# A two-layer decoder trunk on one core: the norms before the query projections rearranged, and two parts of x loaded through the chunk buffers

## The chip, the core and the metric

The kernel runs on one core of a Trainium2 chip. Its time is the device time of one execution in microseconds (us); for a program on one core that is the core's own. Lower is better.

The engines are named as in the profile: PE is TensorE (matrix products; PEld is its loading of weights), DVE is VectorE, ACT is ScalarE, POOL is GpSimd, SP is SyncE, which here only issues transfers. A line such as L293 is line 293 of the kernel before. The changed kernel's lines lie 2 to 25 further down.

## The reference

The input is 256 tokens of width 1024, in float32. Two layers follow each other. Each layer has a token mixer (layer 0 an mLSTM, layer 1 an RG-LRU) beside cross-attention to 256 memory tokens, an output projection, a layer norm, a PEER mixer (a choice among 16384 experts, by query projections and sub-keys), and a second layer norm:

```
for i in range(DEPTH):
    z = x @ w_in[i]
    ...
    mix = concat([mixer(z), cross_attention(z, mem)]) @ w_out[i]
    x = layer_norm(alpha * x + mix, ln1_g[i], ln1_b[i])
    y = peer_ffn(x, peer_w_q[i], peer_subkeys[i], peer_u[i], peer_v[i])
    x = layer_norm(alpha * x + y, ln2_g[i], ln2_b[i])
```

`peer_ffn` begins with `x @ w_q` (1024 to 2048 columns). The norm of concern is the first one of each layer: it stands between the output projection `w_out` and the query projection `w_q`.

## The kernel before

**Precision by splitting.** Every float32 matrix product is made of three products of a rounded type (`mm3`, L166 to L169): each operand is split into a high part H (a cast, ScalarE) and a low part L = value - H (a subtraction, VectorE or GpSimd), and H*H, H*L and L*H are summed in a PSUM bank. One weight chunk (128 rows of a weight, up to 1024 columns) thus gives 24 products of 256 columns in a query projection: eight tiles of 128 columns, three products each.

**The chunk stream.** `plan` lists all weights as chunks in the order of their use. `load` issues their transfers on SyncE's queue into five chunk buffers (`raw`), and `pump` splits the next chunks into three pairs `wH`, `wL`: the cast on ScalarE (L97), and the subtraction either on GpSimd alone (L110), or for the first `pool_cols` columns on GpSimd and for the rest on VectorE (L112). `next()` hands out the split of a chunk and pumps those ahead of it. The gains and biases of a norm (g and b) are chunks too and occupy two of the five buffers until the norm releases them.

**The start.** The first eight chunks of the list are the parts of the transposed x, in turn with the first weight's chunks. A part of x isn't loaded into a chunk buffer but into a piece of `qT` (`to.stage`), a tile that is used for something else later and lies in the memory that two tiles of the setup have used before. The first weight chunks come in two pieces each.

**The norm before the query projection.** `proj_n` runs the last output-projection products in an order written out by hand: those of the first 128 tokens (tt = 0), then those of the second (tt = 1), in three column pieces. Between them the generator `norm` is stepped; it is called with `early` here. For tt = 0 it adds and normalises while the products of tt = 1 run, on VectorE, ScalarE and GpSimd (`scale_beside`, L305 to L309), splits two chunks of the query projection ahead with GpSimd alone doing the low parts (`pool_cols = D`), and turns the first four blocks of 128 columns into the transposed layout (`turn`: transposes on TensorE at L319, high part at L222, low part at L223). For tt = 1 the end of the statistics comes after the last product; then on VectorE: `center` (L293) and `spread` (L298) of the first 256 columns, `turn(1, 0, 1)` for two blocks, and only then the query projection's first product can start. Behind that VectorE does the remaining columns (L293 and L298, 256 and then 512 wide). Their turns follow as side work (`rest`), one step at each later chunk. The norm at the end of layer 0 takes the path `fill`, that at the end of layer 1 the path `last`; neither goes through the lines changed below `if fill`.

**Engines' queues.** Each engine runs its own instructions in the order in which the program issues them (TensorE's weight loads may run ahead of its products), and waits where one depends on another engine.

Of the kernel before, what the change touches and what calls it, by code (L numbers as in the profile page):

```python
# [7 lines left out]
F32 = mybir.dt.float32  # L8
# [5 lines left out]
ALU = mybir.AluOpType  # L14
# [19 lines left out]
EXTRA = 3  # L34
MIX_COLS = 0
GAP = 56
CAND = [(0, 1, 16, 0), (1, 1, 8, 16), (2, 1, 5, 24), (3, 1, 4, 29), (4, 1, 3, 33), (5, 3, 2, 36), (8, 8, 1, 42)]
NCAND = 50
ROWS = [(16, 16), (24, 8), (29, 5), (33, 4), (36, 3), (38, 2), (40, 2), (42, 2)]
# [5 lines left out]
class Trunk:  # L45
# [31 lines left out]
    def pump(self, upto):  # L77
        nc = self.nc
        upto = min(upto, len(self.items))
        while self.n_split < upto:  # L80
            i = self.n_split
            self.load(i + 1)
            ap, n, dest, keep, cuts = self.items[i]
            r = self.loaded.pop(i)
            self.n_split += 1
            if keep is not None:
                self.kept[keep] = r
                continue
            if type(dest) is int:
                h, l = self.extra[dest]  # L90
            elif dest is None:
                h = self.hl.tile([P, D], F32R, name="wH")[:, :n]
                l = self.hl.tile([P, D], F32R, name="wL")[:, :n]
            else:
                h, l = dest()
            for c in cuts:
                (nc.vector.tensor_copy if self.cast_dve else nc.scalar.copy)(h[:, c], r[:, c])  # L97
            k = n if getattr(dest, "pool", False) else min(n, self.pool_cols)
            if len(cuts) > 1:
                for c in cuts:  # L100
                    e = (nc.vector, nc.gpsimd)[c.start > 0]
                    e.tensor_sub(l[:, c], r[:, c], h[:, c].bitcast(F32))
                k = n
            elif k and self.chained:
                nc.vector.tensor_sub(l[:, k:], r[:, k:], h[:, k:].bitcast(F32))  # L105
                k += 2
                nc.gpsimd.tensor_sub(l[:, :k], r[:, :k], h[:, :k].bitcast(F32))  # L107
                k = n
            elif k:
                nc.gpsimd.tensor_sub(l[:, :k], r[:, :k], h[:, :k].bitcast(F32))  # L110
            if k < n:
                nc.vector.tensor_sub(l[:, k:], r[:, k:], h[:, k:].bitcast(F32))  # L112
            self.split[i] = (h, l)
            self.n_flight -= getattr(dest, "stage", None) is None
            self.load(len(self.items))
# [42 lines left out]
            self.tick()  # L158

    pool_cols = MIX_COLS  # L160
    chained = False
    cast_dve = False

# [18 lines left out]
    def proj_n(self, splits, stat, order=range(DT), tail=0, hook=(-1, None)):  # L182
        sH, sL = stat
        parts = [splits, (512, 256, 256) if tail else splits]
        banks = [[self.bank() for _ in p] for p in parts]
        late = []

        def products(tt, k, late):
            t = slice(tt * P, (tt + 1) * P)
            w = parts[tt][k]  # L190
            c0 = sum(parts[tt][:k])
            for n_, dt_, (h, l) in late:
                self.mm3(banks[tt][k][:, :w], sH[:, dt_, t], sL[:, dt_, t], h[:, c0:c0 + w], l[:, c0:c0 + w],
                         n_ == 0, n_ == last[tt])
        last = (DT - 1, DT - 1 - HL_BUFS if tail else DT - 1)
        for n, dt in enumerate(order):
            if n == hook[0]:
                hook[1]()
            late.append((n, dt, self.next(min(HL_BUFS + min(n, EXTRA), DT - n) if tail else HL_BUFS)))
            if n + 1 > DT - tail and n + 1 < DT:  # L200
                continue
            if tail and n + 1 == DT:
                break
            for tt in range(2):
                for k in range(len(parts[tt])):
                    products(tt, k, late)
            late = []
        if not tail:
            return banks
        ln = self.norm(banks, False, True)  # L210
        own, ring = late[:tail - HL_BUFS], late[tail - HL_BUFS:]
        for part in (own, ring):
            for k in range(2):
                products(0, k, part)
        next(ln)
        for k in range(3):
            products(1, k, ring)
        for k in range(3):
            products(1, k, own), next(ln, None)

    def split_to(self, dH, dL, src, cast=None):
        (cast or self.nc.scalar.copy)(dH, src)  # L222
# [31 lines left out]
    def norm(self, y, last, early, fill=False):  # L254
# [40 lines left out]
        def spread(tt, q, n):  # L295
            qs = slice(q * Q, (q + n) * Q)
            xs = x[:, tt, qs]
            nc.vector.scalar_tensor_tensor(xs, xs, rs[:, tt:tt + 1], b[:, qs], op0=ALU.mult, op1=ALU.add)  # L298
# [12 lines left out]
        def store(eng, tt, q, n):  # L311
            qs = slice(q * Q, (q + n) * Q)
            eng.dma_start(self.out[tt * P:(tt + 1) * P, qs], x[:, tt, qs])

        def turn(tt, q, n):
            p = self.bank()
            for j in range(2 * n):
                dt = 2 * q + j
                nc.tensor.transpose(p[:, j * P:(j + 1) * P], x[:, tt, dt * P:(dt + 1) * P], self.ident)  # L319
            t = slice(tt * P, (tt + 1) * P)  # L320
            ds = slice(2 * q, 2 * q + 2 * n)
            self.split_to(self.xH[:, ds, t], self.xL[:, ds, t],
                          p[:, :2 * n * P].rearrange("p (a t) -> p a t", a=2 * n))
# [29 lines left out]
        if early:  # L353
            yield
            part = add(1, 0)
        half(*part)
        self.pool_cols = D
        self.pump(self.n_got + 2 + (2 if early else 1))
        self.pool_cols = MIX_COLS
        if early:  # L360
            turn(0, 0, 2)
# [15 lines left out]
            return  # L377
        center(1, 0, 1)
        root(1)
        spread(1, 0, 1)  # L380
        if not early:
            turn(0, 0, 1)
        turn(1, 0, 1)
        scale(1, 1, 1)
        scale(0, 2, 2), scale(1, 2, 2)
        self.release("g", "b")

        def rest():
            yield
            if not early:  # L390
                turn(0, 1, 1)
            turn(1, 1, 1)
            yield
            turn(0, 2, 2)
            yield
            turn(1, 2, 2)
# [751 lines left out]
    def plan(self):  # L1148
        A = self.A

        def w(name, n, dts=range(DT)):
            for dt in dts:
                self.add(A[name][dt], n)

        def part(name, dst, k):
            fl = lambda t: t[:, 2 * k:2 * k + 2, :].rearrange("p a b -> p (a b)")
            to = lambda: (fl(dst()[0]), fl(dst()[1]))
            to.pool = True
            self.add(A[name][k], 512, to)

        def first(name):
            w(name, 1024, range(3))
            for k in range(4):
                part("memT", lambda: self.mem, k)
                w(name, 1024, (3 + k,))
            w(name, 1024, (7,))

        def norm(n, layer):
            for k in "gb":
                ap = A[f"{n}_{k}"][layer]  # L1170
                self.add(bass.AP(tensor=ap.tensor, offset=ap.offset, ap=[[0, P], [1, D]]), D, None, k)

        def tail(layer):
            for i, dt in enumerate((6, 7, 0, 1, 2, 3, 4, 5)):
                self.add(A["w_out"][layer, dt], D, i - 2 if 0 <= i - 2 < EXTRA else None)
            norm("ln1", layer)
            for g in range(2):
                for dt in range(DT):
                    self.add(A["w_q"][layer, g, dt], D)
            for i in range(P):  # L1180
                self.add(A["u"][layer, i], D)
            for i in range(P):
                e = i - P + HL_BUFS + EXTRA
                self.add(A["v"][layer, i], D, e if layer and 0 <= e < EXTRA else None)
                k = (i - N0 - 4) // 6
                if layer == 0 and i > N0 and (i - N0 - 4) % 6 == 0 and 0 <= k < 8:
                    if k < 4:
                        part("memT", lambda: self.mem, k)
                    else:
                        self.add(A["wkv"][1, k - 4], D, lambda c=k - 4: self.kvw[c])  # L1190
            norm("ln2", layer)
        for dt in range(DT):
            to = lambda dt=dt: (self.xH[:, dt, :], self.xL[:, dt, :])
            to.stage = lambda dt=dt: self.qT[:, dt, :]
            self.add(A["xT"][dt // 2][:, dt % 2 * T:(dt % 2 + 1) * T], T, to)
            self.add(A["w0kg"][dt], 896, cuts=2 if dt < 2 else 1)
        first("w0qx")
        for c in range(4):
            self.add(A["wkv"][0, c], D)
        w("w0v", 768)  # L1200
        w("w0o", 768)
        tail(0)
        w("w1x", 1024)
        w("w1g", 768)
        tail(1)
# [87 lines left out]
```

## Time and profile before

| | us |
|---|---|
| median of 3 runs | 1838.18 |
| lowest and highest | 1837.2 and 1838.45 |
| the profiled execution | 1838.14 |
| its span, first to last instruction | 1836.4 |

| engine | busy us | share of the span |
|---|---|---|
| TensorE, products | 1806.4 | 98% |
| TensorE, weight loads | 1665.8 | 91% |
| VectorE | 1297.5 | 71% |
| ScalarE | 941.4 | 51% |
| GpSimd | 433.1 | 24% |

The trace numbers are start times from the span's beginning and durations, both in us; a line of the timeline reads: start, duration, engine, line of the kernel, operation, output and inputs, shapes, count, and in brackets the idle time before it with what ended it. A granted clock of 1.00 is TensorE's full clock. The norm before the query projection is at 127 to 148 us in layer 0 and at 1025 to 1046 us in layer 1.

### The profile page before, as it was taken

To read this page: it belongs to the slowest core of one execution; us is meant where nothing else is said; L and a number is where in the kernel's file an instruction comes from. 1 tells how busy PE (TensorE), PEld (TensorE's weight loads), DVE (VectorE), ACT (ScalarE), POOL (GpSimd) and SP (SyncE) were. 2 spreads that over 40 slices of the span, in tenths; PEclk is the share of its full clock that TensorE was granted. 3 is DMA by queue.
4 is the path that set the end of the run, shared out by engine and by line. 5 is a ranking of instruction groups with operands and counts; after the bars stand their busy time and mean duration, and the time that the engine had idled before them with its cause. 6 is when DMAs were issued, how large, how long until landed. Compare 5 with 4: busy or idle time off the path is not lost.

```text
span 1836.4 us, 33231 instructions
## 1 busy us (share of the span) xinstructions
PE 1806.4 (98%) x12756; PEld 1665.8 (91%) x12756; DVE 1297.5 (71%) x2652; ACT 941.4 (51%) x1608; POOL 433.1 (24%) x324
## 2 busy tenths in 40 slices
PE   8999999999999999999999899999999999999998
PEld 8999999999999888888898699999999988888886
DVE  5674669599998555666568648795999965555556
ACT  6554555455545444555547355554555455555443
POOL 2005772333331000000011368335333300000000
PEclk9999999999999999999999899999999999999999
DMA  6656566655555666667654355666555566666664
GB/s 235 208 158 187 173 186 194 195 172 162 161 161 164 192 196 193 195 217 226 209 186 133 118 174 183 192 196 187 161 162 161 162 182 194 193 192 193 194 194 137
DMA packets 95265, 334.21 MB, mean 182 GB/s; under 512 B 10621, under 2 KB 13697, under 8 KB 94849
## 3 DMA queue, kind: packets, MB, share of 16 engines
q1 hardware_dynamic: 93464, 328.93, 58.6%
q10 hardware_dynamic: 1640, 3.15, 0.5%
q8 instruction: 100, 1.64, 0.4%
q14 instruction: 61, 0.49, 0.1%
HBM read 330.98 MB, written 1.05 MB: 181 GB/s over the span
## 4 chain that ended last, share of the span: by engine, by line
PE 73%; issue 15%; POOL 7%; DVE 3%; ACT 2%; DMA 0%; POOLq 0%; DVEq 0%; SPq 0%; ACTq 0%
PE bank L167 23%; PE bank L169 23%; PE bank L168 23%; POOL wL L107 7%; PE bank L226 2%; ACT wH L97 1%; DVE wL L112 0%; PE bank L319 0%; DVE aa L765 0%; DVE xc L731 0%; POOL wL L110 0%; DVE st L278 0%; DVE x L272 0%; ACT pr L451 0%; DMA cp<-in_rg_par_dram 0%
## 5 line engine op out<-in xcount | busy, mean ns | idle before, releaser
L97 ACT CAST wH<-raw 128x1024 fp32r<-128x1024 f32 (+2 forms) x605 | 628.6, 1040 | 772.5 <-PE bank L169 323.3
L112 DVE TENSOR_TENSOR wL<-raw,wH 128x1024 fp32r<-128x1024 f32 (+3 forms) x410 | 464.1, 1134 | 452.1 <-ACT wH L97 451.4
L167 PE MATMUL bank<-xHL,wH 128*128 128x256 f32 x2536 | 717.5, 283 | 7.1 <-ACT wH L97 6.2
L169 PE MATMUL bank<-xHL,wL 128*128 128x256 f32 x2536 | 704.5, 278 | 2.2 <-DVE wL L112 2.2
L168 PE MATMUL bank<-xHL,wH 128*128 128x256 f32 x2536 | 704.6, 278 | 0.0
L167 PEld LDWEIGHTS bank<-xHL,wH 128*128 128x128 f32 x2536 | 479.5, 189 | 7.9 <-ACT wH L97 6.2
L169 PEld LDWEIGHTS bank<-xHL,wL 128*128 128x128 f32 x2536 | 479.3, 189 | 3.1 <-DVE wL L112 2.8
L168 PEld LDWEIGHTS bank<-xHL,wH 128*128 128x128 f32 x2536 | 479.9, 189 | 0.3 <-DVE xHL L223 0.3
L168 PE MATMUL bank<-wL,cH 128*128 128x512 f32 x1015 | 394.3, 388 | 0.0
L169 PE MATMUL bank<-wH,cL 128*128 128x512 f32 x1015 | 394.3, 388 | 0.0
L167 PE MATMUL bank<-wH,cH 128*128 128x512 f32 x1015 | 394.3, 388 | 0.0
L110 POOL TENSOR_TENSOR wL<-raw,wH 128x1024 fp32r<-128x1024 f32 (+1 forms) x121 | 259.1, 2145 | 212.8 <-ACT wH L97 212.2
L169 PEld LDWEIGHTS bank<-wH,cL 128*128 128x128 f32 x1015 | 190.5, 188 | 39.7
L167 PEld LDWEIGHTS bank<-wH,cH 128*128 128x128 f32 x1015 | 190.5, 188 | 39.4
L168 PEld LDWEIGHTS bank<-wL,cH 128*128 128x128 f32 x1015 | 190.5, 188 | 39.0
L107 POOL TENSOR_TENSOR wL<-raw,wH 128x386 fp32r<-128x386 f32 x126 | 129.6, 1029 | 280.0 <-DVE wL L105 280.0
L308 POOL TENSOR_TENSOR x<-x,raw 128x256 f32<-128x256 f32 x6 | 4.8, 805 | 556.7 <-ACT x L305 556.7
L929 DVE TENSOR_TENSOR oh<-iota,i12T 128x1024 f16<-128x1024 f16 x128 | 130.2, 1017 | 0.0
L105 DVE TENSOR_TENSOR wL<-raw,wH 128x640 fp32r<-128x640 f32 x126 | 103.9, 825 | 7.7
L932 DVE TENSOR_TENSOR oh<-oh,gT 128x1024 f16<-128x1024 f16 x128 | 90.0, 703 | 4.4
L1062 PE MATMUL bank<-oh 128*128 128x128 f16 x1024 | 80.9, 220 | 1.1 <-DVE oh L932 1.1
L1062 PEld LDWEIGHTS <-oh 128*128 128x128 f16 x1024 | 58.8, 97 | 6.0 <-DVE oh L932 1.5
(273 smaller groups left out, 1527.7 us busy)
## 6 DMA issues: line engine op xcount, KB each, us to landing
raw<-in_u_dram SPq DMA_DIRECT2D x256, 512.0 KB, 3.7
raw<-in_v_dram SPq DMA_DIRECT2D x256, 512.0 KB, 4.3
raw<-in_w_q_dram SPq DMA_DIRECT2D x32, 512.0 KB, 3.8
raw<-in_w_out_dram SPq DMA_DIRECT2D x16, 512.0 KB, 4.5
raw<-in_w0qx_dram SPq DMA_DIRECT2D x8, 512.0 KB, 4.8
raw<-in_wkv_dram SPq DMA_DIRECT2D x8, 512.0 KB, 4.7
raw<-in_w1x_dram SPq DMA_DIRECT2D x8, 512.0 KB, 4.5
raw<-in_w0v_dram SPq DMA_DIRECT2D x8, 384.0 KB, 6.1
```

Source lines behind the costliest of these rows:

```text
L97: (nc.vector.tensor_copy if self.cast_dve else nc.scalar.copy)(h[:, c], r[:, c])
L105: nc.vector.tensor_sub(l[:, k:], r[:, k:], h[:, k:].bitcast(F32))
L107: nc.gpsimd.tensor_sub(l[:, :k], r[:, :k], h[:, :k].bitcast(F32))
L110: nc.gpsimd.tensor_sub(l[:, :k], r[:, :k], h[:, :k].bitcast(F32))
L112: nc.vector.tensor_sub(l[:, k:], r[:, k:], h[:, k:].bitcast(F32))
L167: mm(out, sH, mH, start=start, stop=False, skip_group_check=True)
L168: mm(out, sH, mL, start=False, stop=False, skip_group_check=True)
L169: mm(out, sL, mH, start=False, stop=stop, skip_group_check=True)
L226: self.nc.tensor.matmul(out, lhsT, rhs, start=start, stop=stop, skip_group_check=True)
L929: nc.vector.tensor_tensor(flat(oh[:, 1:3]), self.iota2.unsqueeze(1).to_broadcast([P, 4, P, 2]), pairs(self.i12T[:, j]), op=ALU.is_equal)
L932: nc.vector.tensor_tensor(flat(oh[:, 0:2]), two.rearrange("p z (q e t) -> p z q e t", q=2, t=2), pairs(self.gT[:, j]), op=ALU.mult)
L1062: nc.tensor.matmul(wp[:, qs], oh[:, 2, q // 2, :, q % 2], oh[:, z, q // 2, :, q % 2], start=z == 0, stop=z == 1, skip_group_check=True)
```

## The change

1. In the norm, the second chunk that is split ahead has its low part halved: GpSimd does 512 columns, VectorE the other 512. VectorE's half is put off: it is recorded in a list (`owed`) and issued later, behind the first turn of tt = 1.
2. `spread` of the first 256 columns of tt = 1 is issued as two passes of 128 columns, and `turn1` turns the two blocks one by one: transpose, cast, transpose, cast into one PSUM bank, then the two low parts.
3. `idle` issues transposes of the identity into a bank that nobody reads: 20 ahead of `turn1`, five behind it.
4. The first two parts of x are loaded into chunk buffers and no longer into `qT`.
5. Branches for a norm that is neither `early`, `last` nor `fill` go; no norm of this kernel took them.

```
+FILL = (20, 5)
...
             if k < n:
-                nc.vector.tensor_sub(l[:, k:], r[:, k:], h[:, k:].bitcast(F32))
+                rest = lambda l=l, r=r, h=h, k=k: nc.vector.tensor_sub(l[:, k:], r[:, k:], h[:, k:].bitcast(F32))
+                self.put_off(rest) if self.put_off else rest()
...
+    put_off = None
...
+    def idle(self, n):
+        b = self.bank()
+        for _ in range(n):
+            self.nc.tensor.transpose(b[:, :P], self.ident, self.ident)
...
+        def turn1(tt, *dts):
+            p = self.bank()
+            t = slice(tt * P, (tt + 1) * P)
+            for j, dt in enumerate(dts):
+                nc.tensor.transpose(p[:, j * P:(j + 1) * P], x[:, tt, dt * P:(dt + 1) * P], self.ident)
+                nc.scalar.copy(self.xH[:, dt, t], p[:, j * P:(j + 1) * P])
+            for j, dt in enumerate(dts):
+                nc.vector.tensor_sub(self.xL[:, dt, t], p[:, j * P:(j + 1) * P], self.xH[:, dt, t].bitcast(F32))
...
+        owed = []
         self.pool_cols = D
-        self.pump(self.n_got + 2 + (2 if early else 1))
+        self.pump(self.n_got + 3)
+        if early:
+            self.pool_cols, self.put_off = 512, owed.append
+            self.pump(self.n_got + 4)
+            self.put_off = None
         self.pool_cols = MIX_COLS
...
         center(1, 0, 1)
         root(1)
-        spread(1, 0, 1)
-        if not early:
-            turn(0, 0, 1)
-        turn(1, 0, 1)
+        for dt in range(2):
+            ds = slice(dt * P, (dt + 1) * P)
+            nc.vector.scalar_tensor_tensor(x[:, 1, ds], x[:, 1, ds], rs[:, 1:2], b[:, ds], op0=ALU.mult, op1=ALU.add)
+        self.idle(FILL[0])
+        turn1(1, 0, 1)
+        self.idle(FILL[1])
+        owed.pop()()
         scale(1, 1, 1)
...
         for dt in range(DT):
             to = lambda dt=dt: (self.xH[:, dt, :], self.xL[:, dt, :])
-            to.stage = lambda dt=dt: self.qT[:, dt, :]
+            if dt > 1:
+                to.stage = lambda dt=dt: self.qT[:, dt, :]
```

More of the change, by code (lines that the diff above doesn't have):

```diff
@@ L389, in rest @@
             yield
-            if not early:
-                turn(0, 1, 1)
             turn(1, 1, 1)
```

## The prediction

> **What bounds the kernel now.** I read the page first, then TensorE's list of waits, then the timeline and the table of stretches at the few places where TensorE stands still or runs slowly.
>
> ```profile
> span 1836.4 us, 33231 instructions
> PE 1806.4 (98%) x12756; PEld 1665.8 (91%) x12756; DVE 1297.5 (71%) x2652; ACT 941.4 (51%) x1608; POOL 433.1 (24%) x324
> PE bank L167 <- ACT wH L97: 6.2, 1, 6.2
> PE bank L319 <- DVE x L298: 6.1, 2, 3.4
> ```
>
> TensorE is busy for 98% of the span, so only its idle time and its slow time are to be had. Its two largest waits are the two places that the change touches: 6.2 us once, at the start, and 6.1 us over two norms, both before the first transposes of the second token half (L319). Times in the trace are of one execution: span 1836.4 us, 1838.14 us with what lies around it; the median of the three runs shown is 1838.18, so I subtract from 1838.14 as it stands. About 0.2% (3.7 us, a bound at 1834.5) is what a measurement of this kernel can tell from no change.
>
> The table of stretches shows what each norm costs beyond the wait (columns: length, then busy time of TensorE, weight load, VectorE, ScalarE and GpSimd, the granted clock, DMA share, GB/s):
>
> ```profile
> 137.33:140.74 3.41, 1.03 (x9) 0.82 (x7) 3.24 (x9) 0.29 (x1) 3.41 (x10) 1.00 0.64 149
> 142.13:147.51 5.38, 5.38 (x24) 5.21 (x24) 5.27 (x9) 1.04 (x1) 1.28 (x1) 0.50 0.25 89
> 147.83:150.65 2.82, 2.82 (x26) 2.82 (x25) 1.39 (x3) 1.22 (x2) 1.79 (x1) 1.00 0.88 328
> 1040.17:1045.28 5.11, 5.11 (x22) 4.94 (x23) 5.00 (x7) 1.04 (x1) 1.55 (x3) 0.50 0.29 100
> 973.52:976.93 3.41, 2.33 (x18) 2.13 (x18) 3.41 (x9) 0.84 (x2) 0.00 (x0) 1.00 0.53 156
> 976.93:980.34 3.41, 3.39 (x29) 3.39 (x30) 2.00 (x3) 1.05 (x1) 0.00 (x0) 1.00 0.69 215
> 1014.47:1017.88 3.41, 0.53 (x2) 0.30 (x2) 2.66 (x5) 1.20 (x2) 0.00 (x0) 1.00 0.52 154
> 1017.88:1021.30 3.42, 3.42 (x9) 2.58 (x9) 3.13 (x5) 0.37 (x1) 0.00 (x0) 0.54 0.26 43
> ```
>
> After each norm the first 24 products of the query projection run at clock 0.50: 5.38 us for what takes 2.8 at clock 1.00. The loss is about 2.5 us per norm. A stretch with 1.03 or 0.53 us of work in 3.4 is followed by the half clock; one with 2.33 us is not. So keeping TensorE at work for more than some share between 30% and 68% of such a stretch would keep the clock.
>
> **The start.**
>
> ```profile
> 0.83 0.23 POOL L240 IOTA ji<- 128x128 int32 x1 [0.39 <-POOLq L1282]
> 1.54 0.06 DVE L250 MEMSET eps<- 128x1 f32 x1
> 1.61 0.39 SPq L125 DMA_DIRECT2D qT<-in_xT_dram  x1
> 2.06 0.90 SPq L125 DMA_DIRECT2D raw<-in_w0kg_dram  x2
> 3.95 1.28 ACT L97 ACT_TABLE_LOAD   x1 [3.95 <-DMA qT<-in_xT_dram]
> 5.56 1.03 ACT L97 CAST wH<-raw 128x448 fp32r<-128x448 f32 x2
> 6.17 0.58 PE L167 MATMUL bank<-xHL,wH 128*128 128x256 f32 x1 [6.17 <-ACT wH L97]
> DMA to landing us min/median/max: 3.1/5.1/6.4
> ```
>
> The first transfer, x into qT, starts right behind VectorE's last setup instruction (1.54 to 1.61): qT lies where the setup tiles lay. With the first two parts in chunk buffers, the order as built has no wait on that transfer, and none on ScalarE's table load, which now waits for it. SyncE can then start somewhere between GpSimd's 0.83 and a little before; I take 0.7, 0.9 earlier. The table load (1.28) leaves the path. What is late next is the first weight piece: issued 0.45 behind x, at 1.15, and landing 3.1 later (the least of the weight transfers here), 4.25; its cast takes 0.5, and TensorE starts at 4.8 instead of 6.17: **-1.35**. If the piece lands only 0.9 earlier than ScalarE took it (5.56), the gain is 1.0; if the half-clock time of the start does not move with it, 0.7; if it lands faster, 1.9. Two of five chunk buffers are taken by x until it is split, so the fourth weight chunk waits for that; it queues behind a backlog and I cost it at nothing (at most its own 0.4 us of issue).
>
> **The norms, to the first product.** Row by row in layer 0, then layer 1:
>
> ```profile
> 139.79 0.48 DVE L293 SCALAR_TENSOR_TENSOR x<-x,mv,raw 128x256 f32<-128x256 f32 x1
> 140.38 0.49 DVE L298 SCALAR_TENSOR_TENSOR x<-x,rs,raw 128x256 f32<-128x256 f32 x1
> 141.01 0.66 PE L319 MATMUL bank<-ident,x 128*128 128x128 f32 x2 [2.65 <-DVE x L298]
> 141.71 0.37 ACT L222 CAST xHL<-bank 128x256 fp32r<-128x256 f32 x1 [1.63 <-PE bank L319]
> 142.11 0.42 DVE L223 TENSOR_TENSOR xHL<-bank,xHL 128x256 fp32r<-128x256 f32 x1 [1.25 <-ACT xHL L222]
> 142.13 0.58 PE L167 MATMUL bank<-xHL,wH 128*128 128x256 f32 x1 [0.46 <-ACT xHL L222]
> 150.77 0.60 PE L319 MATMUL bank<-ident,x 128*128 128x128 f32 x4
> 151.33 0.28 PE L168 MATMUL bank<-xHL,wH 128*128 128x256 f32 x1
> 1033.40 4.70 POOL L110 TENSOR_TENSOR wL<-raw,wH 128x1024 fp32r<-128x1024 f32 x2
> 1037.47 0.91 DVE L293 SCALAR_TENSOR_TENSOR x<-x,mv,raw 128x256 f32<-128x256 f32 x1
> 1049.23 0.28 PE L168 MATMUL bank<-xHL,wH 128*128 128x256 f32 x1
> ```
>
> The 20 identity transposes, at 0.11 each (four take 0.60 with their fill time of about 0.27), fill 2.2 of the 2.65 us (layer 0) and of the 3.44 (layer 1) before L319; they end before the data is ready and delay nothing. VectorE's first half spread is ready at about 140.73 instead of 140.87, the first transpose runs from 140.87 and its copy ends at 141.45. But the second transpose writes the bank that this copy reads, and in the order as built it waits for ScalarE: 141.5; its copy ends at 142.1, and both subtractions come behind it. So turning one by one gains nothing to the first product (142.15 for 142.13), and about 0.15 to the second (142.45). The five transposes lie in that wait. In layer 1 one thing more: L293 takes 0.91 instead of 0.48, because it stands until GpSimd's 4.70 us pair ends at 1038.10. With 1.5 chunks that work ends about 1.1 us earlier, before L293: **0.4** gained.
>
> **The norms, after the first product.** If the clock holds, the first chunk's 24 products end at 145.1 instead of 147.66. That is not the gain yet, for VectorE is late next:
>
> ```profile
> 143.32 1.28 POOL L110 TENSOR_TENSOR wL<-raw,wH 128x512 fp32r<-128x512 f32 x1 [1.23 <-ACT wH L97]
> 143.37 1.78 DVE L293 SCALAR_TENSOR_TENSOR x<-x,mv,raw 128x512 f32<-128x512 f32 x1
> 145.19 0.75 DVE L298 SCALAR_TENSOR_TENSOR x<-x,rs,raw 128x512 f32<-128x512 f32 x1
> 147.51 0.69 DVE L112 TENSOR_TENSOR wL<-raw,wH 128x512 fp32r<-128x512 f32 x1
> 147.73 1.05 ACT L97 CAST wH<-raw 128x1024 fp32r<-128x1024 f32 x1 [4.49 <-PE bank L168]
> 149.43 0.42 DVE L223 TENSOR_TENSOR xHL<-bank,xHL 128x256 fp32r<-128x256 f32 x1
> ```
>
> The third chunk of products (151.33) needs the low part that L223 writes at 149.43 to 149.85, at the end of VectorE's row of norm passes and low halves. Before, it had 1.5 us to spare. After, that row holds one low half more (the put-off one, 0.69), and it meets GpSimd twice: L293 took 1.78 instead of 0.75 beside a GpSimd subtraction, 1.03 more. In before, the next GpSimd subtraction comes only when ScalarE's cast at 147.73 follows the end of the first products. With products at the full clock that cast moves to 145.2, GpSimd's subtraction to 146.3, into VectorE's passes. Worked out: subtractions from 142.1 (0.5), put-off half (0.62), two passes of 256 (0.9) with 1.0 blocked, four passes of 512 (2.9) with 1.03 blocked, a copy (0.2), two low halves (1.24), the last subtraction (0.42): 150.9. The third chunk's second product then starts at 150.95 instead of 151.33: **-0.4**. In layer 1 the same steps, counted from L293 at 1037.47 (897.68 behind 139.79, and now without its stall), put that product at 1048.63, against 1049.23: **-0.6**; the 0.4 is in it. From there on both kernels are bound by TensorE alike, and what is gained stays. Of the ends: without the second meeting 1.03 more is gained in each norm (1.4 and 1.6); with a third meeting (the cast behind the second chunk, GpSimd at 149.5, between the two low halves) 1.03 is lost in each, +0.6 and +0.4.
>
> The put-off half also holds its chunk buffer until 143.3, where before GpSimd's pair let go of it. The transfer queued for it feeds a cast at 148.4, five us later, against landings of up to 6.4 at the start when many share the engines; alone I cost it at nothing, and 1 us if it is as slow as there. On GpSimd's queue only the layer's constants and the third chunk stand behind the half that goes, and they come earlier.
>
> Sum: 1838.14 - 1.35 - 0.4 - 0.6 = 1835.8.
>
> **Do identity transposes hold the clock?** No stretch of this trace is filled by transposes alone. For it speaks that a transpose occupies TensorE for as long as any product of 128 columns, 0.11 us, and the stretch at 137.33 would be busy for 3.2 of 3.4 us. Against it: the two real transposes at 141.01, with the products right behind them, did not bring the clock back for another 6.5 us. The Trainium skill ("TensorE: Matmul & The Clock Gate", Part 4, PE-mode transpose) says that transpose mode does not count as busy time in the way products do, so that the full clock does not engage. By that rule the clock would drop as before, and the sum would be near that of the second rival; no row here shows it.
>
> **Rivals.**
>
> *VectorE keeps up.* The second meeting does not happen, because VectorE's passes keep the port or GpSimd comes between them without harm: 1838.14 - 1.35 - 1.4 - 1.6 = 1833.8. For it: one blocked instruction per GpSimd subtraction is all the trace shows. Against it: VectorE's passes run without a gap from 142.1, so whatever GpSimd does falls on one.
>
> *The transposes do not count.* The clock drops at 140.75 as before; the two real transposes and the five idle ones are slow (0.21 each), the first product starts at 142.7, but the second no longer waits, and by the third the two kernels are level: +0.1 per norm, less the 0.4 of layer 1 and the start: 1836.6.
>
> *The third chunk becomes a new stall, and the clock falls there.* With all three meetings TensorE stands from 148.7 to 151.95, 3.2 us, longer than the 2.65 us that dropped the clock before; the half clock then costs 24 x (0.213 - 0.115) = 2.4 us in each norm, moved by one chunk only. 1838.14 - 1.35 + 1.0 + 4.8 = 1842.6, slower. It decides from a stall of about 2 us upward; the forecast's own stall is 2.1, so it is close. Without the clock's fall this case gives 1837.8.
>
> **How the numbers follow.** The forecast has 0.38, VectorE keeping up 0.34, transposes not counting 0.20, the new stall 0.08. The time is the forecast's, 1835.8, whose own range is 1834.5 to 1837.2 (the start's 0.7 to 1.9 and half a meeting either way). The range of 1832.8 to 1838.6 takes in the second case with the start's upper bound, and the others but for the fall of the clock. Faster by over 0.2% needs under 1834.5: 0.85 of the second case, 0.15 of the first, together 0.35, and 0.01 of the third. Slower needs over 1841.9: half of the last case and a hundredth for transfers that come late, 0.05. The rest, 0.59, is within 0.2%.
>
> **What would show it.** In the changed profile: SyncE's first transfer at 0.6 to 0.8 and the first product near 4.8; granted clock 1.00 in the first 24 products of both query projections (0.50: transposes do not count); one VectorE pass of about 1.8 us per GpSimd subtraction, two per norm; TensorE waiting about 2 us at the third chunk for VectorE's subtraction. If that wait is missing, the second case holds; if it is over 3 us with clock 0.50 behind it, the last. I am wrong outright if the first product of either projection starts over 1 us later than before, or if the start gains under 0.5.

## The result, and the profile after

| | before | after |
|---|---|---|
| median, us | 1837.82 | 1840.18 |
| lowest and highest | 1835.75 and 1840.25 | 1835.93 and 1843.21 |
| runs | 20 | 20 |
| the profiled execution | 1838.14 | 1839.58 |

The ratio of after to before is 1.0014, with a 95% interval of 1.0007 to 1.0020: about 2.4 us slower, where 1835.8 was forecast and 1838.6 was the upper end of the range. The runs of after also lie much further apart (7.3 us) than those of before (4.5).

The page of after, first lines:

```profile
span 1837.8 us, 33345 instructions
PE 1808.8 (98%) x12806; PEld 1668.8 (91%) x12806; DVE 1303.8 (71%) x2658; ACT 941.9 (51%) x1610; POOL 429.4 (23%) x324
```

TensorE is busy 2.4 us longer than before. Its list of waits (total, times, longest):

```profile
PE bank L171 <- DVE xHL L232: 5.5, 2, 2.8
PE bank L170 <- ACT wH L98: 4.6, 1, 4.6
PE bank L328 <- DVE x L405: 1.0, 2, 0.7
```

Both waits of before have shrunk as meant: 6.2 to 4.6 us at the start, and 6.1 to 1.0 over the two norms, now that identity transposes stand in them (another 0.7 there is the second transpose waiting for the copy out of its bank). A new one is on top: twice 2.8 us, between the first product of the third weight chunk (L170) and the second (L171), for a low part that VectorE writes at L232. (The lines of the changed kernel lie 1 to 25 further down: L98, L111, L113 and L232 here are L97, L110, L112 and L223 of before.)

The timeline at the start, and then around the norm of layer 0, the rows in order of time:

```profile
0.73 1.28 ACT L98 ACT_TABLE_LOAD   x1 [0.73 <-PEq L1307]
0.74 0.39 SPq L127 DMA_DIRECT2D raw<-in_xT_dram  x1
1.18 0.90 SPq L127 DMA_DIRECT2D raw<-in_w0kg_dram  x2
4.01 1.17 ACT L98 CAST wH<-raw 128x448 fp32r<-128x448 f32 x2 [0.57 <-DMA raw<-in_w0kg_dram]
4.62 0.58 PE L170 MATMUL bank<-xHL,wH 128*128 128x256 f32 x1 [4.62 <-ACT wH L98]
...
138.25 0.49 DVE L302 SCALAR_TENSOR_TENSOR x<-x,mv,raw 128x256 f32<-128x256 f32 x1
139.99 0.33 PE L328 MATMUL bank<-ident,x 128*128 128x128 f32 x1 [0.36 <-ACT xHL L329]
140.62 0.36 PE L170 MATMUL bank<-xHL,wH 128*128 128x256 f32 x1
141.00 0.38 PE L171 MATMUL bank<-xHL,wH 128*128 128x256 f32 x1
141.98 1.32 POOL L111 TENSOR_TENSOR wL<-raw,wH 128x512 fp32r<-128x512 f32 x1 [2.50 <-ACT wH L98]
142.18 1.40 DVE L307 SCALAR_TENSOR_TENSOR x<-x,rs,raw 128x256 f32<-128x256 f32 x1
144.99 1.85 POOL L111 TENSOR_TENSOR wL<-raw,wH 128x512 fp32r<-128x512 f32 x1 [1.69 <-ACT wH L98]
145.73 1.66 DVE L307 SCALAR_TENSOR_TENSOR x<-x,rs,raw 128x512 f32<-128x512 f32 x1
147.14 0.36 PE L170 MATMUL bank<-xHL,wH 128*128 128x256 f32 x1
147.52 2.35 DVE L113 TENSOR_TENSOR wL<-raw,wH 128x512 fp32r<-128x512 f32 x2
148.03 1.29 POOL L111 TENSOR_TENSOR wL<-raw,wH 128x512 fp32r<-128x512 f32 x1 [1.19 <-ACT wH L98]
149.79 0.41 DVE L232 TENSOR_TENSOR xHL<-bank,xHL 128x256 fp32r<-128x256 f32 x1
150.25 0.39 PE L171 MATMUL bank<-xHL,wH 128*128 128x256 f32 x1 [2.75 <-DVE xHL L232]
...
1038.71 0.48 DVE L302 SCALAR_TENSOR_TENSOR x<-x,mv,raw 128x256 f32<-128x256 f32 x1
```

VectorE has no gap from 140.66 to 151.4, and three of its instructions take longer than elsewhere, each beside a GpSimd subtraction (a meeting, below): L307 of 256 columns 1.40 instead of 0.48, L307 of 512 columns 1.66 instead of 0.75, and the pair of low halves 2.35 instead of the 1.28 that it takes where no subtraction falls on it (in the kernel without the put-off half, below). So the row meets GpSimd three times before L232 comes, and TensorE stands from 147.5 to 150.25.

The table of stretches. The ends are set to the steps of the granted clock, which in all these traces lie on a grid of 3.413 us (in after from 151.24 to 1018.23 are 254 such steps):

```profile
137.59:141.00 3.41, 2.71 (x21) 2.11 (x19) 2.10 (x8) 0.97 (x4) 1.88 (x13) 1.00 0.27 111
141.00:144.42 3.42, 3.42 (x29) 3.42 (x30) 3.35 (x6) 1.45 (x2) 1.32 (x1) 1.00 0.56 161
147.83:151.24 3.41, 0.98 (x8) 0.99 (x9) 3.41 (x5) 0.61 (x2) 1.29 (x1) 1.00 0.87 267
151.24:154.66 3.42, 3.42 (x18) 3.42 (x18) 0.16 (x1) 0.06 (x1) 0.00 (x0) 0.50 1.00 388
1045.54:1048.95 3.41, 2.36 (x21) 2.16 (x19) 3.37 (x5) 1.57 (x3) 2.22 (x2) 1.00 0.51 145
1048.95:1052.36 3.41, 1.71 (x14) 1.71 (x15) 2.85 (x4) 0.00 (x0) 0.77 (x1) 1.00 0.86 274
```

The identity transposes keep the stretch ahead of the first products busy (2.71 us of 3.41), and these now run at the full clock (141.00). But the stall leaves 0.98 us of work in one stretch, 29%, and the next runs at 0.50. In layer 1 the same stall of 2.75 us falls across two stretches, which keep 69% and 50%, and the clock stays.

Where the time went, in the profiled executions: the first norm begins 1.54 us earlier (138.25 for 139.79). From there to ScalarE's next table load (L1046 in before, at 197.36 and, in layer 1, 1095.23) layer 0 takes 60.36 us instead of 57.57, and the same stretch of layer 1 58.08 instead of 57.76. -1.54 + 2.79 + 0.32, and -0.13 over the rest, are the 1.44 between the two executions. A number from a single execution also holds some chance: in the eight profiled executions with the new start the first norm begins 1.2 to 2.3 us earlier than in before, and in the norms alone, which have the old start, 0.5.

### The profile page after: what moved, and what is told of

Same layout as the page of the kernel before. It is cut to its first block, busy times and chain, and to the rows that moved or that the text cites. A ratio compares the mean times of both kernels' runs of the same rounds, so it can differ in the third digit from the quotient of the medians.

```text
span 1837.8 us, 33345 instructions
## 1 busy us (share of the span) xinstructions
PE 1808.8 (98%) x12806; PEld 1668.8 (91%) x12806; DVE 1303.8 (71%) x2658; ACT 941.9 (51%) x1610; POOL 429.4 (23%) x324
## 5 line engine op out<-in xcount | busy, mean ns | idle before, releaser
L98 ACT CAST wH<-raw 128x1024 fp32r<-128x1024 f32 (+2 forms) x605 | 628.7, 1040 | 775.9 <-PE bank L172 320.2
L113 DVE TENSOR_TENSOR wL<-raw,wH 128x1024 fp32r<-128x1024 f32 (+3 forms) x412 | 467.3, 1137 | 448.0 <-ACT wH L98 447.3
L170 PE MATMUL bank<-xHL,wH 128*128 128x256 f32 x2536 | 716.2, 282 | 4.6 <-ACT wH L98 4.6
L171 PE MATMUL bank<-xHL,wH 128*128 128x256 f32 x2536 | 703.4, 277 | 5.5 <-DVE xHL L232 5.5
L171 PEld LDWEIGHTS bank<-xHL,wH 128*128 128x128 f32 x2536 | 478.3, 189 | 6.3 <-DVE xHL L232 5.9
L170 PEld LDWEIGHTS bank<-xHL,wH 128*128 128x128 f32 x2536 | 477.5, 188 | 4.6 <-ACT wH L98 4.6
L171 PE MATMUL bank<-wL,cH 128*128 128x512 f32 x1015 | 394.3, 388 | 0.0
L170 PE MATMUL bank<-wH,cH 128*128 128x512 f32 x1015 | 394.3, 388 | 0.0
L111 POOL TENSOR_TENSOR wL<-raw,wH 128x1024 fp32r<-128x1024 f32 (+1 forms) x121 | 255.8, 2116 | 219.3 <-ACT wH L98 218.5
L170 PEld LDWEIGHTS bank<-wH,cH 128*128 128x128 f32 x1015 | 190.5, 188 | 39.6
L171 PEld LDWEIGHTS bank<-wL,cH 128*128 128x128 f32 x1015 | 190.5, 188 | 39.3
```

What stands on the lines that cost most here:

```text
L113: rest = lambda l=l, r=r, h=h, k=k: nc.vector.tensor_sub(l[:, k:], r[:, k:], h[:, k:].bitcast(F32))
L170: mm(out, sH, mH, start=start, stop=False, skip_group_check=True)
L171: mm(out, sH, mL, start=False, stop=False, skip_group_check=True)
```

## The experiments

The theory (A in the expectations): the start's gain is real; the norms lose it, because VectorE's row with three meetings ends late and TensorE's stall for it also drops the clock in part of the executions. The rivals put the loss elsewhere: in the earlier start, in the put-off half, in the turning one by one or in later transfers. Each kernel was timed beside the kernel before; before took 1837.68 beside the kernels of the start, the transposes, the filled stall and the GpSimd share, and 1837.84 beside the other four. The two stretches are those of the last paragraph, each in one profiled execution.

| kernel | median, us | ratio to before, 95% | wait at the third chunk, layers 0 and 1 | stretch 0 | stretch 1 |
|---|---|---|---|---|---|
| before | 1837.8 | | none | 57.57 | 57.76 |
| after | 1840.18 | 1.0007 to 1.0020 | 2.75, 2.75 | 60.36 | 58.08 |
| start only | 1835.27 | 0.9984 to 1.0002 | none | 56.46 | 56.87 |
| norms only | 1841.81 | 1.0012 to 1.0035 | 2.82, 2.75 | 58.21 | 58.08 |
| no identity transposes | 1836.78 | 0.9986 to 1.0004 | none | 58.00 | 57.56 |
| stall filled | 1837.41 | 0.9989 to 1.0007 | 0.64, 0.57 | 58.22 | 58.07 |
| no put-off half | 1835.82 | 0.9979 to 0.9997 | 1.33, 1.26 | 56.65 | 57.02 |
| no GpSimd share | 1834.08 | 0.9972 to 0.9990 | 0.99, 0.92 | 56.38 | 56.31 |
| reordered | 1832.93 | 0.9963 to 0.9983 | 0.48, 0.41 | 55.87 | 55.73 |
| both | 1830.96 | 0.9951 to 0.9978 | none | 55.05 | 55.14 |

### The start alone, and the norms alone

On the kernel before, only this:

```
-            to.stage = lambda dt=dt: self.qT[:, dt, :]
+            if dt > 1:
+                to.stage = lambda dt=dt: self.qT[:, dt, :]
```

> The kernel before with the change of the start alone (the first two parts of x through the chunk buffers). Theory A (the whole loss is made at the norms, where VectorE comes late for the third chunk and the clock falls in the stall): the first product at 4.6 us as in the changed kernel, the lead of 1.5 us is still there at the second norm, and the time is 1.2 to 1.6 us below that of the kernel before. Rival (the start's chunk buffers upset later transfers and the lead is given back): within 0.5 us of the kernel before.

And the reverse of these lines in the changed kernel:

> The start of the changed kernel is undone (all parts of x go through qT again), both norms stay as changed. Theory A (the start's lead is real and kept, the loss is all in the norms: a stall of about 2.8 us before the second product of the third chunk, and the half clock behind it): the first product at about 6.2 us, no lead at layer 0's norm, the same two stalls of 2.7 to 2.9 us, and a time about 1.5 us above the whole change, 1841.5 plus or minus 1 on a chip where the kernel before takes 1837.7. Rival (the earlier start, or x in the chunk buffers, is part of what is lost): 1839.5 or less, or stalls under 2 us.

The start alone took 1835.27, 2.4 us under before by the medians and 1.3 by the ratio of 0.9993 (the interval just reaches 1); 1.2 to 1.6 was expected. The norms alone took 1841.81 (1841.5 expected), 4.0 above before and 1.6 above after; 1.54 was the start's lead in after's trace. Within the intervals the two parts add up, and the rival that the start is part of the loss falls. The norms alone stall as after does, but in the profiled execution the clock did not fall:

```profile
146.99:150.40 3.41, 1.49 (x14) 1.29 (x12) 3.41 (x4) 1.53 (x2) 2.26 (x2) 1.00 0.55 166
150.40:153.82 3.42, 2.52 (x21) 2.52 (x22) 2.04 (x4) 0.00 (x0) 0.00 (x0) 1.00 0.99 314
1048.11:1051.52 3.41, 1.93 (x16) 1.93 (x17) 2.63 (x4) 0.00 (x0) 0.54 (x1) 1.00 0.87 270
```

Same stall, but the grid lies so that its stretches keep 44%, 74% and 57% of work (1.49, 2.52 and 1.93 of 3.41). That execution took 1838.52; the seven runs go from 1837.62 to 1845.1. So two costs can be told apart: against before's profiled execution the norm with its stall, but without a fall of the clock, costs 58.21 - 57.57 = 0.64 in layer 0 and 0.32 in layer 1, and a fall 60.36 - 58.21 = 2.15. Of the 2.15, 1.5 arise in the slow stretch (151.24 to 154.66). The rest comes behind it, where after's products follow each other at 0.118 us until 172 us and those of the norms alone at 0.113, at a granted clock of 1.00 in both; why is open. Nor is 0.64 firm: before's norm itself took 57.57 in one execution and, with the same code, 56.46 in the start alone.

### No identity transposes

`FILL = (20, 5)` becomes `FILL = (0, 0)`.

> The changed kernel with FILL = (0, 0): no identity transposes, all else as it is. Theory A: the clock falls in the wait ahead of the first products as it did before, the first 24 products take about 5.1 us, VectorE is then in time for the third chunk (its wait there under 0.5 us), and the norms cost what they did before to within 0.5 us each; with the start's lead the time is 0.5 to 2 us below the kernel before, so 3 to 4 us below the changed kernel. Rival (the put-off half and the turning one by one make the loss, whatever the clock does): the wait at the third chunk stays over 2 us and the time stays above that of the kernel before.

```profile
140.43:143.84 3.41, 2.85 (x14) 2.79 (x14) 3.10 (x6) 1.29 (x2) 1.30 (x1) 0.50 0.39 91
```

The first products are slow again, as in before, and the wait for L232 is gone: while TensorE is slow, VectorE has time. Theory A's numbers hold. In layer 0 L232 ends 10.0 us behind the norm's first pass (11.95 in after), because ScalarE's cast for the next weight chunk waits for the slower products, GpSimd's next subtraction starts at 147.32, and only one meeting falls ahead of L232. At 1836.78 the kernel is 3.4 under after. So turning one by one and the put-off half do little harm while the products are slow (1.5 over the start alone, with intervals that overlap); the harm is that faster products both ask for the low part earlier and bring GpSimd's subtractions onto the row that makes it.

### The stall filled

Twenty more identity transposes, in the bank of `turn(0, 2, 2)` and ahead of its real transposes, which TensorE reaches just before the third chunk:

```
-        def turn(tt, q, n):
+        def turn(tt, q, n, fill=0):
...
+            for _ in range(fill):
+                nc.tensor.transpose(p[:, :P], self.ident, self.ident)
...
-            turn(0, 2, 2)
+            turn(0, 2, 2, 20)
```

> The changed kernel with 20 more identity transposes, issued ahead of the turn of the third step (into the bank of that turn, before the real transposes), so that they lie in the wait of about 2.8 us ahead of the third chunk's second product. Theory A: VectorE's lateness stays, so the second product of that chunk starts as late as now, but the clock no longer falls behind it; the time goes down by the clock's part alone, about 1 to 2.4 us for both norms in the mean, to about the kernel before (1837 to 1839), and the runs spread less than the 7 us of the changed kernel. Rival (the clock's fall in that stall is worth little, the stall itself is the whole loss): no change beyond 0.5 us.

```profile
147.05 2.35 PE L336 MATMUL bank<-ident 128*128 128x128 f32 x20
150.59 0.39 PE L171 MATMUL bank<-xHL,wH 128*128 128x256 f32 x1 [0.64 <-DVE xHL L232]
147.03:150.44 3.41, 2.92 (x27) 2.72 (x25) 3.41 (x5) 1.62 (x2) 1.50 (x2) 1.00 0.79 234
150.44:153.86 3.42, 3.27 (x28) 3.27 (x29) 1.30 (x3) 0.34 (x2) 0.00 (x0) 1.00 0.97 359
```

The second product of the third chunk starts as late as in after (12.0 us behind the norm's first pass in both), but the clock stays at 1.00 behind it, the time is 1837.41, and the runs lie within 2.5 us instead of 7.3. The 2.8 us between after and this kernel are therefore the clock's share of the loss, a little more than the 1 to 2.4 expected. Its stretches (58.22, 58.07) are those of the norms alone without a fall.

The mean granted clock of every run is on record too, and says the same. The 20 runs of after, by that mean:

| mean granted clock | runs of after | their mean time, us |
|---|---|---|
| 0.998 | 2 | 1837.0 |
| 0.997 | 6 | 1838.3 |
| 0.996 | 5 | 1840.6 |
| 0.995 | 7 | 1842.0 |

One slow stretch of 3.41 us lowers the mean over some 1838 us by 0.0009, so a row is about one slow stretch more than the row above it. With the stall filled all 11 runs lie at 0.997 or 0.998.

### No GpSimd share

GpSimd is left out of the low parts of the four chunks behind the two that are split ahead; VectorE does them whole:

```
+            self.pool_cols = POOL_COLS
...
-            self.pool_cols = POOL_COLS
+            self.pool_cols = 0
```

> The changed kernel with GpSimd's share taken away in the four weight chunks behind the two that are split ahead: VectorE makes their whole low parts (1.22 instead of 0.69 us each), so none of its norm passes meets a GpSimd subtraction. Theory A (three meetings of about 1 us each make VectorE late): no norm pass over 0.8 us; the low part for the third chunk is ready 3 - 1.06 = about 1.9 us earlier, the wait there falls from 2.75 to about 0.9 us, the clock holds, and the time is 1834 to 1836.5. Rival (VectorE's own work is what is late, the put-off half above all): the wait grows by the 1.06 us to 3.8 and the time rises by 1 to 3 us.

```profile
145.25 2.35 DVE L113 TENSOR_TENSOR wL<-raw,wH 128x1024 fp32r<-128x1024 f32 x2
147.99 0.38 PE L171 MATMUL bank<-xHL,wH 128*128 128x256 f32 x1 [0.99 <-DVE xHL L232]
```

No pass of VectorE is over 0.75 us, though VectorE does more: its pair of low parts has 2048 columns now and takes the 2.35 that 1024 took beside GpSimd. The wait falls to 0.99, the time to 1834.08, under both kernels and as expected. The meetings are the larger part of the lateness.

### No put-off half

Both chunks split ahead go to GpSimd alone again, as in before.

```
-        self.pump(self.n_got + 3)
-        if early:
-            self.pool_cols, self.put_off = 512, owed.append
-            self.pump(self.n_got + 4)
-            self.put_off = None
+        self.pump(self.n_got + (4 if early else 3))
...
-        owed.pop()()
```

> The changed kernel without the put-off half: both weight chunks split ahead are subtracted whole on GpSimd, as before the change. Theory A (the put-off half is 0.6 us of the lateness, the meetings with GpSimd are the rest): the wait at the third chunk falls to 2.1 to 2.2 us and three meetings stay, layer 1's first spread pass is back at about 0.9 us, and the time is 1838 to 1840 beside 1837.7 of the kernel before. Rival (the put-off half is what makes the third chunk late): a wait of less than 1 us, and a time under 1836.

```profile
146.94 1.28 DVE L113 TENSOR_TENSOR wL<-raw,wH 128x512 fp32r<-128x512 f32 x2
148.09 1.27 POOL L111 TENSOR_TENSOR wL<-raw,wH 128x512 fp32r<-128x512 f32 x1 [1.82 <-ACT wH L98]
148.14 0.41 DVE L232 TENSOR_TENSOR xHL<-bank,xHL 128x256 fp32r<-128x256 f32 x1
148.47 1.44 DVE L113 TENSOR_TENSOR wL<-raw,wH 128x512 fp32r<-128x512 f32 x1
148.60 0.39 PE L171 MATMUL bank<-xHL,wH 128*128 128x256 f32 x1 [1.33 <-DVE xHL L232]
```

Neither expectation holds whole. The wait is 1.33, not 2.1 nor under 1, and the time 1835.82, better than the theory said and just inside the rival's "under 1836". The rows tell why: without the put-off half's 0.62 us the pair of low halves (1.28) is all but through when GpSimd starts at 148.09, and the third meeting hits the low half behind L232 (1.44), which nobody is waiting for yet. So the half costs twice, its own time and the place of a meeting. In layer 1 the norm's first pass, the centring one (the expectation calls it the spread pass), took 0.91 again.

### Reordered

In the changed kernel one pass pair over 512 columns, which is needed only for a later chunk, moves behind the turn whose low part the third chunk waits for:

```
-        scale(0, 2, 2), scale(1, 2, 2)
-        self.release("g", "b")
+        scale(0, 2, 2)
...
             turn(1, 1, 1)
+            scale(1, 2, 2)
+            self.release("g", "b")
```

> The changed kernel with one pass of 512 columns and the layer's last one, scale(1,2,2) with its release of g and b, moved behind the transposes turn(1,1,1). VectorE's row ahead of L232 for the third chunk loses two passes (1.5 us) and the meeting that falls on them. Theory A: that subtraction ends 2 to 2.3 us earlier, TensorE waits 0.8 us or less for it, the clock stays at 1.00 there, and the time is 1833.5 to 1836 beside 1837.7 of the kernel before. Rival (the lateness is set elsewhere, or g and b, released some 3 us later, hold up the next layer's constants and the weights behind them): the wait stays above 1.5 us, or a new wait for a transfer or a low part of a weight takes its place, and the time is above 1837.

```profile
147.40 0.41 DVE L232 TENSOR_TENSOR xHL<-bank,xHL 128x256 fp32r<-128x256 f32 x1
147.73 0.74 DVE L302 SCALAR_TENSOR_TENSOR x<-x,mv,raw 128x512 f32<-128x512 f32 x1
147.87 0.39 PE L171 MATMUL bank<-xHL,wH 128*128 128x256 f32 x1 [0.48 <-DVE xHL L232]
```

L232 comes 2.3 us earlier against the norm's first pass (9.20 behind it, 11.54 in after), the wait is 0.48, the clock stays, and the time is 1832.93, below the expected 1833.5 to 1836. The later release of g and b makes no new wait. The rival falls.

### Both

The last change and "No GpSimd share" together.

> The reordered kernel (scale(1,2,2) behind turn(1,1,1)), and besides no GpSimd share in the four chunks behind the two that are split ahead. Theory A: no meeting and a shorter row, so TensorE does not wait at the third chunk in either norm (under 0.3 us), against 1.0 us in each with the GpSimd share taken away alone; 1832 to 1833.5 beside 1837.7 of the kernel before, about 1 to 2 us under that kernel's 1834.1. Rival (something else is late next, such as the low part of the weight, now VectorE's alone, or the last transposes): the same time as that kernel within 0.5 us, with another wait in TensorE's list.

```profile
143.52 2.35 DVE L113 TENSOR_TENSOR wL<-raw,wH 128x1024 fp32r<-128x1024 f32 x2
145.79 0.42 DVE L232 TENSOR_TENSOR xHL<-bank,xHL 128x256 fp32r<-128x256 f32 x1
146.56 0.28 PE L171 MATMUL bank<-xHL,wH 128*128 128x256 f32 x1
```

The low part is ready 0.35 us before TensorE asks for it. No wait is left there in either norm, and the stretches are 2.5 and 2.6 us shorter than before's. That is about the loss which the prediction put on the half clock behind each norm (5.38 us for 2.8). The median is 1830.96, 0.9964 of before (0.9951 to 0.9978), below the expected 1832 to 1833.5; the five runs lie within 0.75 us.

## Why the prediction was wrong

**The start: right.** SyncE's first transfer at 0.74 (0.7 predicted), the weight piece issued at 1.18 (1.15), the first product at 4.62 (4.8), a lead of 1.54 at the first norm (1.35, with 1.9 as upper end). What was late next was the weight piece, as said. That the lead is so close is in part luck, since it was 1.2 to 2.3 in the executions with this start.

**Identity transposes hold the clock: right.** The first products ran at 1.00 in both norms, and without the transposes at 0.50. The rule of the Trainium skill ("TensorE: Matmul & The Clock Gate", Part 4, PE-mode transpose), that transpose mode does not count as busy time in the way products do, is not borne out here: twenty transposes of 2.35 us kept the full clock, in the norms and again in the filled stall. The profile lists them as matrix products with the identity, so whether they are in the mode that is meant there isn't shown.

**To the first product: right.** 2.37 us from the norm's first pass to the first product (2.36 predicted, 2.34 before) and 2.75 to the second (2.66). The second transpose does wait for the copy out of its bank, 0.36. In layer 1 the first pass took 0.48 instead of 0.91.

**VectorE's row: the step that failed.** The term "Worked out: ... 150.9" counts two meetings with GpSimd ahead of the third chunk's low part; there were three, in both layers. Counted from the norm's first pass, L232 was to end at 11.1 and ended at 11.95. The difference is the third meeting: 1.07 (2.35 for 1.28), less 0.2 of small errors. The prediction named it, but as an end of the range ("with a third meeting (the cast behind the second chunk, GpSimd at 149.5, between the two low halves)"). Its own terms decide it: they put the two low halves at 149.25 to 150.49, so a subtraction starting at 149.5 falls on them. In after it started at 148.03, which is 149.57 less the lead of 1.54. The row and GpSimd's time were both right; the sum was taken without what they give together. Its own price for a third meeting, +0.6 and +0.4 per norm in place of -0.4 and -0.6, is what the profiled executions then showed (+0.64 and +0.32); so close a match is luck, as before's norm alone varies by 1.1.

**The clock behind the stall: failed with it, and costs more.** The forecast had a stall of 2.1 us, called it close to where the clock falls, and put the fall at nothing in the sum. The gap was 2.75, and the fall cost 2.8 us in the medians. Of the 4.4 us by which the forecast missed, that is the larger part; the other is the row, with which the two norms lost about 1.0 where 1.0 was to be gained. The case with the chance of 0.08, "The third chunk becomes a new stall", is what happened: it had TensorE standing from 148.7 to 151.95, which with the lead taken off is 147.16 to 150.41, and the trace has 147.50 to 150.25. Its two times, 1837.8 without the clock's fall and 1842.6 with one in each norm, bracket the measured 1840.18. They were taken as alternatives; the runs from 1835.93 to 1843.21 hold both kinds, as their mean clocks of 0.995 to 0.998 show. In the profiled executions the fall depended on where the stall lay on the grid; where in the kernel the other runs' slow stretches lay isn't known.

**The put-off half's buffer and the transfers: right at nothing.** No wait for a transfer appeared in the norms, nor when g and b were released later still.

## What to carry to other kernels

When a stall is removed, lay every queue's new times side by side, and check each instruction against what then runs beside it: two rows that are each right can still meet. Filling a wait moves the bound to the next engine, here VectorE's order of work; two passes moved out of that row's way and GpSimd kept off it turned 2.4 us lost into 6.9 gained. A clock that falls in some executions and not in others makes a stall's price a chance, so judge it by many runs, their spread and their mean clock, not by one profile.

## What the runs showed of the hardware

The granted clock is 1.00 or 0.50 in these traces and changes only on a grid of 3.413 us whose place differs from run to run. The Trainium skill ("TensorE: Matmul & The Clock Gate", Part 1, What's actually happening) has a free-running window of 3413 ns, and the traces agree (3.4133). Around these norms, stretches with 40% or less of TensorE's time busy were followed by 0.50, those with 44% or more kept 1.00. So it is not the length of a gap alone that counts: after's two stalls have the same 2.75 us, one in one stretch (29% busy), one across two (69% and 50%). And at 0.50 the clock rose behind a slow stretch only where that was nearly full:

```profile
137.54:140.95 3.41, 0.82 (x7) 0.61 (x6) 3.15 (x9) 0.29 (x1) 3.41 (x10) 1.00 0.68 156
140.95:144.37 3.42, 2.90 (x11) 2.36 (x12) 2.22 (x4) 1.42 (x2) 2.19 (x9) 0.50 0.70 189
144.37:147.78 3.41, 3.41 (x18) 3.41 (x17) 3.34 (x6) 0.05 (x1) 0.23 (x1) 0.50 0.03 10
```

Those are before's; here the start alone, with the same code at the norm (these ends lie 0.06 us behind the grid, hence 0.99 and 0.51):

```profile
136.06:139.48 3.42, 0.59 (x4) 0.20 (x2) 2.52 (x8) 0.43 (x2) 3.42 (x15) 0.99 0.77 183
139.48:142.89 3.41, 3.12 (x13) 2.96 (x14) 3.07 (x5) 1.28 (x2) 1.76 (x5) 0.51 0.44 162
142.89:146.30 3.41, 3.41 (x32) 3.41 (x31) 3.38 (x6) 1.32 (x2) 0.86 (x1) 1.00 0.30 56
```

In before the slow stretch was 85% busy (2.90 of 3.42) and a second slow one followed; here it was some 90% and the clock came back, and the layer's stretch is 1.1 us shorter (56.46 for 57.57) without a change of the code there. These shares are read from ten traces, with matmul ends that are modelled; elsewhere, at 1019 to 1024 us, three stretches with 58 to 60% were also followed by 0.50, while one with 60% at 1030 us in the start alone kept 1.00, so between 40% and 60% the busy share alone does not decide. No run varied it by itself.
